# Context ahead through the mixer, the gated unit and the second feed-forward step of a fp32 trunk, with the latent's scan beside

## The chip, the cores and the metric

The kernel runs on one core of a Trainium2 chip. The core has a matrix engine (PE in the profile), a vector engine (DVE), a scalar engine (ACT), GpSimd (POOL) and a queue engine for transfers (SP). Each works through its own instructions in order; semaphores tie them together. The metric is device time of one execution in microseconds, median of three runs.

## The reference

A trunk of two layers for one sample: 512 latent tokens and 256 context tokens, width 1024, all in fp32. Each layer is a half feed-forward step, a token mixer and another half step; each part begins with an RMS norm whose scale, shift and gate come from a conditioning vector (the adaptive norm). The mixer of layer 0 is a diagonal state space model (S5) in both directions; that of layer 1 is gated linear attention (GLA).

```python
def ffn_half_step(x, w_norm, shift, scale, gate, w_in, w_out):
    h = rmsnorm(x, w_norm) * (1.0 + scale) + shift
    return x + 0.5 * gate * swiglu_ffn(h, w_in, w_out)
...
    yc_f, hf_re, hf_im = s5_direction(uc, *fwd, h0, h0)
    yc_b, hb_re, hb_im = s5_direction(jnp.flip(uc, 1), *bwd, h0, h0)
    yx_f, _, _ = s5_direction(ux, *fwd, hf_re, hf_im)
    yx_b, _, _ = s5_direction(jnp.flip(ux, 1), *bwd, hb_re, hb_im)
...
        z = jnp.einsum('bld,de->ble', jax.nn.gelu(y), w_glu.astype(F32)) + b_glu.astype(F32)
        val, gate = jnp.split(z, 2, axis=-1)
        return (val * jax.nn.sigmoid(gate)).astype(h.dtype)
```

The latent's scan starts from context's last states (`hf`, `hb`). Nothing goes from the latent to context before the GLA mixer, which needs both.

## The kernel before

**Layout.** The trunk (`xT`) lies with the width on 128 partitions in 8 tiles and the 768 tokens along the free dimension: 0 to 255 context, 256 to 767 latent. Every large product is three matmuls (`mm3`, L109): each operand is split into a rounded part and a rest (`hi`, `lo`), and hi*hi, lo*hi and hi*lo are summed. A weight tile of 512 KB is loaded by SP into `wraw` (4 buffers), cast on ACT into `whi` (L88, 5 buffers) and subtracted on DVE into `wlo` (L89, 5 buffers). The normed activation is kept split in `h`.

**Order.** A scheduler sets each engine's order from the order of the code and pool buffers; the code can hand a stage a list of *fillers*, pieces of other work that are issued between its units. `ffn` (L221) goes through 22 hidden units of 128: per unit a gate and a value product (16 `mm3` for each stretch of tokens), SiLU and their product, and in groups the output product. Two to three stretches of tokens share each weight. Adaptive-norm vectors come in 36 blocks of 2 MB of weights: one way on PE (`ten`, L394 and L401), one as a filler on DVE (`by_vector`, L422: `vec`, `rest`).

**The stages.** Loads; first half step of layer 0 (with the preparation of the S5 factors as fillers); S5; gated unit; second half step; first half step of layer 1; GLA; last half step; norm and store.

**S5.** The tokens are taken in runs of 8 (32 of context, 64 of the latent). `inputs` (L764) writes the normed input through DRAM (`U`). `states` (L796, matmuls L811) gives the state that each run adds. `scan` (L819, operations at L499) runs over the 96 runs on DVE: at each step the last state times the factors, and two additions, for each direction apart: 6 operations. `lagged` (L838, L851) adds what the tokens of a run give each other; its tables come from DRAM (`T`) and are cast on ACT (L845). `outputs` (L855) takes, for each of 8 tiles, copies of the states on ACT and DVE (L885, `xs`), 16 matmuls (L906) with a loaded factor (`O`), a sum (L908), a gelu (L910) and a store through DRAM (`Y`). `glu` (L916) loads Y (`yk`, 3 buffers), splits it (L931 on ACT, L932 on DVE) and makes 8 units of 16 `mm3` for each of two halves of 384 tokens. Nine adaptive blocks are made on PE around the scan (`ten`).

## Time and profile before

| what | value |
|---|---|
| median of 3 runs | 2896.99 us (2893.2 to 2899.43) |
| profiled execution, its own time | 2895.71 us |
| its span | 2893.9 us |
| PE busy | 95% of the span, mean granted clock 0.97 |
| DMA | 305.44 MB, mean 106 GB/s |

The page gives busy time by engine, the span in 40 slices of 72 us, the chain of work that ended last, and groups of instructions by line. The chain view names who was waited for. The timeline gives instructions with their start. A PE record's duration holds its way through the pipeline, so how fast products go is read from the distance of their starts. An fp32 matmul that is not split leaves two records, and a split one leaves one.

### The profile page before, as it was taken

To read this page: it belongs to the slowest core of one execution; us is meant where nothing else is said; L and a number is where in the kernel's file an instruction comes from. 1 tells how busy PE (TensorE), PEld (TensorE's weight loads), DVE (VectorE), ACT (ScalarE), POOL (GpSimd) and SP (SyncE) were. 2 spreads that over 40 slices of the span, in tenths; PEclk is the share of its full clock that TensorE was granted. 3 is DMA by queue.
4 is the path that set the end of the run, shared out by engine and by line. 5 is a ranking of instruction groups with operands and counts; after the bars stand their busy time and mean duration, and the time that the engine had idled before them with its cause. 6 is when DMAs were issued, how large, how long until landed. Compare 5 with 4: busy or idle time off the path is not lost.

```text
span 2893.9 us, 44979 instructions
## 1 busy us (share of the span) xinstructions
PE 2750.2 (95%) x18319; PEld 2589.0 (89%) x18319; DVE 1733.4 (60%) x3980; ACT 874.0 (30%) x1415; POOL 8.7 (0%) x41
## 2 busy tenths in 40 slices
PE   6999999996679999999999999999999899799997
PEld 5899999995479999999999999999998788788887
DVE  6689686536873564555527745575367786643434
ACT  4222222224572322111124221121255453422221
POOL 0000000000000000000000000000000000000000
PEclk9999999997789999999999999999999899899998
DMA  6445343517863133332321433343102111243320
GB/s 224 144 114 146 112 135 121 170 59 234 299 201 84 52 103 88 95 95 88 95 59 37 139 95 103 109 122 90 53 17 87 45 59 59 72 123 93 95 77 30
DMA packets 396044, 305.44 MB, mean 106 GB/s; under 512 B 57994, under 2 KB 344188, under 8 KB 395836
## 3 DMA queue, kind: packets, MB, share of 16 engines
q1 hardware_dynamic: 382908, 289.97, 33.7%
q10 hardware_dynamic: 12928, 12.59, 1.3%
q8 instruction: 144, 2.36, 0.4%
q14 instruction: 64, 0.52, 0.1%
HBM read 275.77 MB, written 30.41 MB: 106 GB/s over the span
## 4 chain that ended last, share of the span: by engine, by line
PE 90%; DVE 3%; DMA 3%; ACT 3%; issue 1%; SPq 0%; ACTq 0%; DVEq 0%
PE bank L113 27%; PE bank L114 27%; PE bank L115 27%; PE bank L811 1%; DMA wraw<-in_ffn_w_in_dram 1%; PE bank L1105 1%; PE bank L1104 1%; PE bank L1106 1%; PE aux L1237 1%; DVE big L499 1%; ACT xs L885 1%; PE aux L690 1%; DVE st L499 1%; PE bank L906 0%; PE bank L394 0%
## 5 line engine op out<-in xcount | busy, mean ns | idle before, releaser
L114 PE MATMUL bank<-h,whi 128*128 128x384 f32 (+3 forms) x3160 | 1048.8, 333 | 1.7 <-DVE h L932 1.7
L115 PE MATMUL bank<-h,wlo 128*128 128x384 f32 (+3 forms) x3160 | 1047.9, 332 | 0.0
L113 PE MATMUL bank<-h,whi 128*128 128x384 f32 (+3 forms) x3160 | 1044.5, 334 | 3.2 <-ACT whi L88 1.7
L88 ACT CAST whi<-wraw 128x1024 fp32r<-128x1024 f32 x313 | 327.7, 1048 | 992.3 <-PE bank L114 960.4
L113 PEld LDWEIGHTS bank<-h,whi 128*128 128x128 f32 (+1 forms) x3160 | 593.3, 189 | 24.7 <-issue 2.3
L114 PEld LDWEIGHTS bank<-h,whi 128*128 128x128 f32 (+1 forms) x3160 | 595.1, 188 | 20.0 <-DVE h L932 2.4
L115 PEld LDWEIGHTS bank<-h,wlo 128*128 128x128 f32 (+1 forms) x3160 | 593.4, 188 | 17.8 <-issue 0.8
L89 DVE TENSOR_TENSOR wlo<-wraw,whi 128x1024 fp32r<-128x1024 f32 x313 | 381.1, 1219 | 277.0 <-ACT whi L88 269.6
L114 PE MATMUL bank<-ml,whi 128*128 128x384 f32 (+2 forms) x1360 | 444.5, 328 | 0.0
L113 PE MATMUL bank<-mh,whi 128*128 128x384 f32 (+2 forms) x1360 | 442.7, 329 | 1.4 <-DVE er L503 1.4
L115 PE MATMUL bank<-mh,wlo 128*128 128x384 f32 (+2 forms) x1360 | 443.7, 328 | 0.0
L264 DVE TENSOR_TENSOR sg<-sg,bank 128x384 f32<-128x384 f32 (+2 forms) x166 | 89.5, 539 | 398.0 <-PE bank L115 385.1
L275 DVE SCALAR_TENSOR_TENSOR xT<-bank,hg,xT 128x256 f32<-128x256 f32 (+3 forms) x488 | 230.2, 500 | 154.4 <-PE bank L115 153.7
L113 PEld LDWEIGHTS bank<-mh,whi 128*128 128x128 f32 x1360 | 255.3, 188 | 8.5 <-issue 1.9
L115 PEld LDWEIGHTS bank<-mh,wlo 128*128 128x128 f32 x1360 | 255.6, 188 | 6.5 <-issue 0.2
L114 PEld LDWEIGHTS bank<-ml,whi 128*128 128x128 f32 x1360 | 255.6, 188 | 6.2
L422 DVE SCALAR_TENSOR_TENSOR adaacc<-wraw,cs,adaacc 128x512 f32<-128x512 f32 x266 | 187.4, 745 | 19.9 <-DMA wraw<-in_ada_w_dram 19.4
L265 ACT CAST mh<-sg 128x384 fp32r<-128x384 f32 (+2 forms) x166 | 83.5, 503 | 326.0 <-DVE sg L264 323.5
L263 ACT ACTIVATE sg<-bank 128x384 f32<-128x384 f32 (+2 forms) x166 | 79.5, 479 | 195.4 <-PE bank L115 195.3
L266 DVE TENSOR_TENSOR ml<-sg,mh 128x384 fp32r<-128x384 f32 (+2 forms) x166 | 89.7, 540 | 28.0 <-ACT mh L265 28.0
L150 ACT ACTIVATE sq<-xT 128x256 f32<-128x256 f32 (+1 forms) x126 | 52.9, 429 | 75.4 <-DVE xT L275 53.9
L151 DVE TENSOR_TENSOR ssq<-ssq,sq 128x256 f32<-128x256 f32 (+1 forms) x126 | 54.9, 437 | 30.6 <-ACT sq L150 27.9
(297 smaller groups left out, 2360.3 us busy)
## 6 DMA issues: line engine op xcount, KB each, us to landing
wraw<-in_ffn_w_in_dram SPq DMA_DIRECT2D x176, 512.0 KB, 3.8
wraw<-in_ada_w_dram SPq DMA_DIRECT2D x97, 512.0 KB, 3.7
wraw<-in_ffn_w_out_dram SPq DMA_DIRECT2D x88, 512.0 KB, 3.5
wraw<-in_gla_w_in_dram SPq DMA_DIRECT2D x24, 512.0 KB, 3.9
s5R<-s5r ACTq DMA_DIRECT2D x16, 512.0 KB, 2.6
s5O<-s5g SPq DMA_DIRECT2D x64, 128.0 KB, 2.4
wlo<-in_ada_w_dram SPq DMA_DIRECT2D x16, 512.0 KB, 10.9
wraw<-in_s_w_glu_dram SPq DMA_DIRECT2D x16, 512.0 KB, 4.8
```

The source lines that it names most:

```text
L88: nc.scalar.copy(out=hi[:, :n], in_=raw[:, :n])
L89: nc.vector.tensor_tensor(out=lo[:, :n], in0=raw[:, :n], in1=hi[:, :n].bitcast(F32), op=ALU.subtract)
L113: mm(out, wh, a[0], start=first, stop=False)
L114: mm(out, wh, a[1], start=False, stop=False)
L115: mm(out, wl, a[0], start=False, stop=last)
L263: nc.scalar.activation(sg, banks[0][:, :e - s], AF.Silu)
L264: nc.vector.tensor_mul(sg, sg, banks[1][:, :e - s])
L265: nc.scalar.copy(out=mh[:, o], in_=sg)
L266: nc.vector.tensor_tensor(out=ml[:, o], in0=sg, in1=mh[:, o].bitcast(F32), op=ALU.subtract)
L275: nc.vector.scalar_tensor_tensor(out=self.xT[:, d, a:z], in0=b[:, a - s:z - s], scalar=gate[i][:, d:d + 1], in1=self.xT[:, d, a:z], op0=AL ...
L422: nc.vector.scalar_tensor_tensor(out=acc[:, v], in0=w[:, k], scalar=col, in1=acc[:, v], op0=ALU.mult, op1=ALU.add)
L499: self.c.nc.vector.tensor_tensor(out=out, in0=a, in1=b, op=op)
```

## The change

1. **Tiles by kind.** `h`, and the scratch that shares its place, are two tiles each, for context (`h0`) and latent (`h1`). `at` picks the one. Stretches that mixed the two kinds, halves of 384, are now 256 and 512 tokens in all stages.
2. **Scan.** One step takes both directions at once: 3 operations, of 256 and twice 128 columns.
3. **Order.** Context's scan (31 steps) stands between the states of the two kinds; then come `lagged`, `outputs` of context, `glu` of context with three latent scan steps behind each of its 8 units, context's norm with two adaptive blocks on PE, and the second half step for context alone. Its fillers are 10 times four scan steps and the 8 pieces of the latent's outputs, whose `O` tiles have their own pool (`om`, 3 buffers). Then `glu` and half step for the latent alone, with the next norm of context as a filler.
4. **Weights.** Those of `glu` and of the second half step, and `O`, are loaded twice, and the former two also cast and subtracted twice.
5. **Adaptive blocks.** By vector in the first half step 8 instead of 4; on PE around S5 4 instead of 9; in the second half step 8 instead of 6; in layer 1's first half step 8 instead of 9.

```diff
-            for z in range(2):
-                def state(s, step=64):
-                    return fview(r, s * P + z * 32 + (64 if step < 0 else 0), [(step, 2), (1, 32)])
-                t = pool.tile([P, 2, 2, 32], F32, tag="st", name="st", bufs=4)
-                self.tt(t, fview(self.sa, z * 32, [(P, 2), (64, 2), (1, 32)]),
-                        state(s - 1).unsqueeze(1).to_broadcast([P, 2, 2, 32]), ALU.mult)
-                self.tt(state(s), state(s), t[:, 0], ALU.add)
-                self.tt(state(s, -64), state(s, -64), t[:, 1], ALU.add)
+            t = pool.tile([P, 2, 2, 64], F32, tag="st", name="st", bufs=2)
+            carry = [fview(self.r[1], o, [(64 - 2 * o, 2), (1, 64)]) for o in (0, 64)]
+            last = carry[0] if s == NX5 else state(s - 1)
+            self.tt(t, fview(self.sa, 0, [(P, 2), (64, 2), (1, 64)]), last.unsqueeze(1).to_broadcast([P, 2, 2, 64]), ALU.mult)
+            new = carry if s == NX5 - 1 else [state(s), state(s, -64)]
+            self.tt(new[0], state(s), t[:, 0], ALU.add)
+            self.tt(new[1], new[1], t[:, 1], ALU.add)
...
         for j in range(KT):
             ws.append([c.weight(wg[:, :, q * D + j * P:q * D + (j + 1) * P]) for q in range(2)])
-            if j < KT - 3:
-                for s, e in parts:
-                    step(j, ws[j], s, e)
+            if j < KT - nlast:
+                step(j, ws[j], *whole)
+            if j < len(work):
+                work[j]()
...
-        both, halves = (0, TOK), [(0, 384), (384, 768)]
+        both, halves = (0, TOK), [(0, CTX), (CTX, TOK)]
...
-            ada = [vec(0, m, q, sp) for m in (4, 3) for q in range(2)]
+            ada = [vec(0, m, q, sp) for m in (4, 3, 5, 7) for q in range(2)]
...
-            s5.scan(sp, NX5, N5)
-            ten(2)
             s5.lagged()
-            ten(2)
-            work = s5.outputs(sp, 3, yp, last)
-            ten(4)
-            work()
+            work = s5.outputs(0, sp, 3, core.spare)
+            ten(1)
+            for f in work:
+                f()
+        mods.scale(0, 2)
+        with pool("s5l") as sp, pool("s5m", "right") as mp:
...
+            def behind(s, e):
+                norm(0, 2, 1, 1)(s, e)
+                ten(2)
+                mods.half_gate(0, 1)
+            s5.glu(0, sp, [(0, CTX)], 0, behind, [lambda: steps(3)] * KT)
+            def beside():
...
+                return [lambda: steps(4)] * 10 + s5.outputs(1, sp, 1, unit)
+            ffn(0, 1, (0, CTX), [(0, CTX)], [(0, CTX)], [(0, CTX)], mp, beside)
...
-            s5.glu(yp, halves, thirds, norm(0, 2, 12))
+            with pool("s5y", "right") as yp:
+                s5.glu(1, yp, lat, 3, norm(0, 2, 12))
             with pool("mid") as mp:
-                ffn(0, 1, both, thirds, halves, thirds, mp,
-                    lambda: rest(6, mp) + [lambda: (mods.scale(1, 0), mods.half_gate(1, 0))], norm(1, 0))
+                ffn(0, 1, (CTX, TOK), lat, [(CTX, TOK)], lat, mp,
+                    lambda: rest(8, mp) + [lambda: (mods.scale(1, 0), mods.half_gate(1, 0)),
+                                           lambda: norm(1, 0, 7, 3)(0, CTX)], norm(1, 0))
```

In the rows below, each is a line of the program, an operation, the tile written and the tiles read, and the shape; lines of the changed kernel differ by some 7 from those before (the scan's operations are L499 before and L506 after, the casts L88 and L89 in both).

DVE, in the scan, before: each step is two products (`st`) and four additions into the state (`big`), with nothing else between them here.

```order
L499 TENSOR_TENSOR st<-s5sa,big 128x128 x2
L499 TENSOR_TENSOR big<-big,st 128x2x32 x4
L499 TENSOR_TENSOR st<-s5sa,big 128x128 x2
L499 TENSOR_TENSOR big<-big,st 128x2x32 x4
L499 TENSOR_TENSOR st<-s5sa,big 128x128 x2
```

DVE, after, in context's second half step (L271 and L273 are its gating, `s` the latent's states):

```order
L89 TENSOR_TENSOR wlo<-wraw,whi 128x1024
L506 TENSOR_TENSOR s_6382<-s_6382,st 128x128
L271 TENSOR_TENSOR sg<-sg,bank 128x256
L506 TENSOR_TENSOR s_6382<-s_6382,st 128x2x64
L506 TENSOR_TENSOR st<-s5sa,s_6382 128x256
L89 TENSOR_TENSOR wlo<-wraw,whi 128x1024
L506 TENSOR_TENSOR s_6382<-s_6382,st 128x128
L273 TENSOR_TENSOR ml<-sg,mh 128x256
L506 TENSOR_TENSOR s_6382<-s_6382,st 128x2x64
L506 TENSOR_TENSOR st<-s5sa,s_6382 128x256
```

The scan's three operations now stand between the subtractions and gatings on which that stage's products wait.

PE, after, where the gated unit of context has ended and its second half step begins (L401: adaptive blocks, here `wraw`, `whi` and `wlo` hold their weights; L171 and L190: the norm's sum and spread):

```order
L401 MATMUL bank<-wraw,cs 32x512 x2
L401 MATMUL bank<-whi,cs 32x512 x2
L401 MATMUL bank<-wlo,cs 32x512 x2
L408 MATMUL aux<-quarter,adar 128x2 x8
L171 MATMUL aux<-ones,ssq 128x1 x2
L190 MATMUL bank<-ident,rs 128x128 x2
L113 MATMUL bank<-h_8302,whi 128x256 x4
L114 MATMUL bank<-h_8302,whi 128x256
```

Before, PE went straight from the last output matmuls (L906) to the gated unit, and the blocks stood ahead of both. Now the blocks and the norm stand between two stages of products, in one queue.

ACT, after, later in that half step (L896: copies of the latent's states; L910: gelu; L270 and L272: gating):

```order
L88 CAST whi<-wraw 128x1024
L272 CAST mh<-sg 128x256
L896 COPY xs_9228<-s_6382 64x4x64 x8
L910 ACT_TABLE_LOAD
L910 ACTIVATE y_10983<-y_10983 128x512
L74 DMA s5Y_846<-y_10983 128x8x64
L270 ACT_TABLE_LOAD
L270 ACTIVATE sg<-bank 128x256
L88 CAST whi<-wraw 128x1024 x2
```

The latent's output pieces have moved in between the casts and gatings of this stage, with a change of the function table on either side of the gelu.

More of the change, by code (lines that the diff above doesn't have):

```diff
@@ L49, in __init__ @@
         self.tmp = stack.enter_context(tc.tile_pool(name="tmp", bufs=1))
-        self.queue = []
-        self.ones = self.const.tile([P, P], F32, name="ones")
+        self.queue, self.h = [], [None, None]
+        self.ones = self.const.tile([P, 1], F32, name="ones")
         nc.vector.memset(self.ones, 1.0)
@@ L484, in __init__ @@
         self.U = [dram.tile([KT, P, L5, n], F32, name=f"s5U{i}") for i, n in enumerate((NX5, N5 - NX5))]
-        self.Y = dram.tile([KT, P, L5, N5], F32, name="s5Y")
+        self.Y = [dram.tile([KT, P, L5, n], F32, name=f"s5Y{i}") for i, n in enumerate((NX5, N5 - NX5))]
     def small(self, name):
@@ L708, in turn_k @@
         def turn_k():
-            b, k = c.aux(), pool.tile([P, 256], F32, tag="s5k", name="s5kt", bufs=1)
+            b, k = c.aux(), c.tmp.tile([P, 384], F32, tag="nt", name="s5kt", bufs=2)[:, :256]
             for z in range(2):
@@ L853, in lagged, with outputs @@
                 nc.scalar.copy(out=u.rearrange("p g n -> p (g n)"), in_=b[:, :4 * N5])
-    def outputs(self, pool, ahead, yp, last):
-        c, nc, r = self.c, self.c.nc, self.r
-        loaded, self.ys = {}, []
+    def outputs(self, kind, pool, ahead, unit):
+        c, nc, r = self.c, self.c.nc, self.r[kind]
+        n0, n = ((0, NX5), (NX5, N5 - NX5))[kind]
+        loaded = {}
         def load(kt):
-            om = [c.spare() for _ in range(2)]
+            om = [unit() for _ in range(2)]
             for z in range(2):
@@ L867, in outputs @@
             loaded[kt] = load(kt)
-        xs = [pool.tile([P, 2, 8, N5], F32, name=f"xs{i}", tag=f"xs{i}", bufs=1) for i in range(2)]
-        for x in xs:
-            nc.gpsimd.memset(x[:, 0, :, 0:1], 0.0)
-        def states(kt, s0, s1, copies):
+        xs = [pool.tile([P, 2, 8, n], F32, name=f"xs{i}", tag=f"xs{i}", bufs=1) for i in range(2)]
+        if kind == 0:
+            for x in xs:
+                nc.gpsimd.memset(x[:, 0, :, 0:1], 0.0)
+                nc.gpsimd.memset(x[:, 1, :, n - 1:n], 0.0)
@@ L889, in outputs @@
-        early = 80
-        with c.tc.issue_after(last.ins):
-            for kt in range(2):
-                states(kt, 0, early, [nc.scalar.copy] * 2)
-        def work():
-            for kt in range(KT):
-                x = xs[kt % 2]
-                om = loaded.pop(kt) if kt in loaded else load(kt)
-                states(kt, early if kt < 2 else 0, N5, [nc.scalar.copy, nc.vector.tensor_copy])
-                y = pool.tile([P, 8, N5], F32, tag="y5", name="y5", bufs=4)
-                for h in range(2):
-                    b = c.bank()
-                    for i in range(4):
-                        g = 4 * h + i
-                        o = b[:, i * N5:(i + 1) * N5]
-                        for z in range(2):
-                            nc.tensor.matmul(o, om[z][:, g * P:(g + 1) * P], x[:, z, g], start=(z == 0), stop=(z == 1))
-                    yh = y[:, 4 * h:4 * h + 4].rearrange("p g n -> p (g n)")
-                    nc.vector.tensor_tensor(out=yh, in0=b[:, :4 * N5], op=ALU.add,
-                                            in1=self.u[kt][:, 4 * h:4 * h + 4].rearrange("p g n -> p (g n)"))
-                    nc.scalar.activation(yh, yh, AF.Gelu_apprx_tanh)
-                c.store(dview(self.Y, kt * P * TOK, [(N5, P), (C5 * TOK, 8), (1, N5)]), y)
-                if 0 < kt < 4:
-                    self.load_y(yp, kt - 1)
@@ L914, in outputs @@
-        return work
-    def glu(self, pool, parts, last, after):
+                    for z in range(2):
+                        at, step, to = (count - 1, -P, 0) if z else (0, P, n - count)
+                        src = fview(r, at * P + a * 64 + z * 32 + 4 * kt, [(1, 4), (step, count)], 64 * g, 64)
+                        dst = fview(x, z * 8 * n + g * n + to, [(2 * n, 4), (1, count)], 64 * a, 64)
+                        (nc.vector.tensor_copy if z and not kind else nc.scalar.copy)(out=dst, in_=src)
@@ new lines, in piece @@
+        def piece(kt):
+            x = xs[kt % 2]
+            om = loaded.pop(kt) if kt in loaded else load(kt)
+            states(kt)
+            y = pool.tile([P, 8, n], F32, tag="y5", name="y5", bufs=2)
+            b = c.bank()
+            for g in range(8):
+                for z in range(2):
+                    nc.tensor.matmul(b[:, g * n:(g + 1) * n], om[z][:, g * P:(g + 1) * P], x[:, z, g],
+                                     start=(z == 0), stop=(z == 1))
+            nc.vector.tensor_tensor(out=y, in0=b[:, :8 * n].rearrange("p (g n) -> p g n", g=8), op=ALU.add,
+                                    in1=self.u[kt][:, :, n0:n0 + n])
+            nc.scalar.activation(y, y, AF.Gelu_apprx_tanh)
+            c.store(dview(self.Y[kind], kt * P * L5 * n, [(n, P), (C5 * L5 * n, 8), (1, n)]), y)
@@ L1099, in proj_v @@
             b = c.bank()
-            ts = slice(t * P, (t + 1) * P)
+            s, e = t * P, (t + 1) * P
             for k in range(KT):
@@ L1490, in hybrid_trunk @@
         factors = held.enter_context(pool("s5c"))
-        blocks = [(0, m, q) for m in (5, 7, 6, 8) for q in range(2)] + \
+        blocks = [(0, m, q) for m in (6, 8) for q in range(2)] + \
                  [(1, m, q) for m in (1, 0, 2, 4, 3, 5, 7, 6, 8) for q in range(2)]
```

127 lines of the change are left out of this document (64 added, 63 removed).

## The prediction

> **What bounds the kernel now.** I read the busy totals first, then the 40 slices, then the chain of work that ended last, then windows by stage.
>
> ```profile
> PE 2750.2 (95%) x18319; PEld 2589.0 (89%) x18319; DVE 1733.4 (60%) x3980; ACT 874.0 (30%) x1415; POOL 8.7 (0%) x41
> PE   6999999996679999999999999999999899799997
> PE 90%; DVE 3%; DMA 3%; ACT 3%; issue 1%; SPq 0%; ACTq 0%; DVEq 0%
> ```
>
> PE carries 90% of the chain and is full in every slice but the first, three from 650 us on, and a few late ones. So time can be won in the holes, and everything added to a full stage is paid in full. The windows (columns: stretch; busy us of PE, of PE's weight loads, of DVE, ACT and POOL with counts; granted clock; DMA share; GB/s) size them:
>
> ```profile
> 100.00:640.00 540.00, 538.62 (x3458) 525.11 (x3457) 390.65 (x919) 127.31 (x197) 3.69 (x7) 1.00 0.44 127
> 640.00:870.00 230.00, 164.45 (x2417) 137.06 (x2417) 172.09 (x782) 135.81 (x218) 1.47 (x12) 0.81 0.75 233
> 848.00:870.00 22.00, 18.62 (x90) 17.51 (x89) 20.29 (x24) 18.72 (x25) 0.00 (x0) 0.84 1.02 282
> 1060.00:1540.00 480.00, 480.00 (x2838) 478.11 (x2837) 243.51 (x405) 96.65 (x144) 0.00 (x0) 1.00 0.30 88
> ```
>
> The hole is the S5 mixer. The timeline gives its ends: the last matmul of the first feed-forward step, the first and last scan operation, and the first matmul of the gated unit.
>
> ```profile
> 660.65 0.28 PE L115 MATMUL bank<-mh,wlo 128*128 128x256 f32 x1
> ...
> 700.55 0.29 DVE L499 TENSOR_TENSOR st<-s5sa,big 128x128 f32<-128x128 f32 x1 [0.33 <-ACT big L816]
> ...
> 810.26 0.23 DVE L499 TENSOR_TENSOR big<-big,st 128x64 f32<-128x64 f32 x1
> ...
> 847.80 0.42 PE L113 MATMUL bank<-h,whi 128*128 128x384 f32 x1
> ```
>
> 847.8 - 660.65 = 187 us pass without a wide product. In the 22 us behind it PE is busy 18.62 at a clock of 0.84, some 15.6 of full-speed work, so another 6 go: **193 us**. The scan takes 110 of them.
>
> **The scan.** Both directions in one operation: 3 per step where there were 6.
>
> ```profile
> L499 DVE TENSOR_TENSOR big<-big,st 128x64 f32<-128x64 f32 x380 | 60.3, 214 | 0.8 <-ACT big L816 0.5
> L499 DVE TENSOR_TENSOR st<-s5sa,big 128x128 f32<-128x128 f32 x190 | 46.1, 280 | 2.3 <-ACT big L816 2.2
> ...
> 661.75 0.41 DVE L151 TENSOR_TENSOR ssq<-ssq,sq 128x256 f32<-128x256 f32 x1
> ```
>
> The timeline merges and overlaps these operations by about 0.08 us: 190 of 0.28 and 380 of 0.214 fill 95 steps at 2 x 0.20 + 4 x 0.135 = 0.94 us. The new step is one operation of 256 columns (0.41 - 0.08 = 0.33) and two of 128 (0.20 each): 0.73 us. Context's 31 steps are 23 us, the latent's 64 are 47.
>
> **The hole after the change.** Context's path no longer holds the latent's 64 steps nor five of nine adaptive-norm blocks, but it still holds the context states (until 700.55), the lag products and context's outputs.
>
> ```profile
> 713.17 10.27 DMA wraw<-s5T
> ...
> 752.31 7.23 PE bank L851 x48
> ...
> 846.97 0.39 PE L906 MATMUL bank<-xs,wraw 128*128 128x96 f32 x2
> 847.19 0.39 PE L906 MATMUL bank<-xs,whi 128*128 128x96 f32 x2
> ...
> s5Y<-y ACTq DMA_DIRECT2D x8, 384.0 KB, 6.5
> yk<-s5Y SPq DMA_DIRECT2D x8, 384.0 KB, 4.6
> u<-s5U SPq DMA_DIRECT2D x7, 128.0 KB, 4.6
> ```
>
> The lag products end at 759.5 now, behind the loads of the lag tables and their ACT copies. With less adaptive-weight traffic they may end at 750; I take 755. Context's 128 output matmuls follow at 0.22 each (two rows start 0.22 apart, one matmul of two records), 28.2 us, to 783. Then add and gelu (1 us), the store of Y (between 4.6, as 128 KB take, and 6.5; taken 4.6), its load (4.6) and the split (about 1.4) give 795. The gated unit's first unit takes its operand tiles one by one, so seven eighths of its 5.7 us run before: effective 790, plus 2 for the low clock at the start. The hole is then 792 - 660.65 = 131 us: **-62**. Bounds: at before's output pace (40 us from 808 to 848, 5 per tile instead of 3.5) and lag products at 759.5 it is -46; with lag products at 745 and the Y transfers half hidden, -77.
>
> **Latent outputs inside full PE.** They go from the hole into context's feed-forward step: 128 matmuls of 64 columns, while the 128 of 32 stay. The trace shows no 64 column case. From above it is bounded by the 0.22 of 96 columns, from below by one column:
>
> ```profile
> 1550.82 0.50 PE L163 MATMUL aux<-ones,ssq 128*128 128x1 f32 x4
> 1551.17 0.69 PE L182 MATMUL bank<-ident,rs 128*128 128x128 f32 x4
> ```
>
> Four records of one column take 0.35 us, 0.09 each, where 96 columns take 0.11: width hardly counts. I take the upper end: **+28** (bounds 22 and 28). The Trainium skill, "TensorE: Matmul & The Clock Gate", section LDWEIGHTS, says that loading a 128-column stationary tile takes 128 / 1.2 GHz, 107 ns, whatever else the matmul does. The trace agrees with 0.09 to 0.11 per record. If cost went with moved columns instead, the split would be free and this term 28 x 64 / 96 = 19.
>
> **Products at other widths.** Gated unit and second step run context and latent apart, 256 and 512 columns, and other stages drop 384.
>
> ```profile
> 619.81 0.34 PE L115 MATMUL bank<-h,wlo 128*128 128x384 f32 x1
> 619.98 0.34 PE L113 MATMUL bank<-h,whi 128*128 128x384 f32 x1
> ...
> 625.93 0.28 PE L114 MATMUL bank<-ml,whi 128*128 128x256 f32 x1
> 626.05 0.28 PE L115 MATMUL bank<-mh,wlo 128*128 128x256 f32 x1
> ```
>
> Starts lie 0.175 apart for 384 columns and 0.118 for 256, both 0.46 ns a column: 0.
>
> **Junction 1, gated unit to feed-forward on context.** Nothing else fills PE here. The sum over the last unit, square sums, the reciprocal root, its spread and the first tile's split follow one another, and PE's queue holds 16 products of two adaptive blocks ahead of the norm's. The trace has one bare norm, at the end of the second step: products stop with the rows just shown, at 1550.8, and start again at 1555.1:
>
> ```profile
> 759.53 3.59 PE bank L394 x32
> ...
> 1555.12 1.43 PE L113 MATMUL bank<-h,whi 128*128 128x256 f32 x5 [0.27 <-ACT h L218]
> ```
>
> so 5 us is the least. On top come the blocks (their 32 records took 3.6 us at 759.5), their weights, which wait for gated-unit slots, and scan operations between the norm's on DVE: **+12** (5 to 22). That old bubble goes, since context's norm is now done beside the latent's products: **-5**.
>
> **Junction 2, feed-forward on context to the latent's gated unit.** The first load of the latent's Y overlays the mid tiles, so on SP it waits for the last matmul of context's step. Three buffers serve eight tiles: load 4.6, split 1.16 + 1.08,
>
> ```profile
> L931 ACT CAST h<-yk 128x512 fp32r<-128x512 f32 x8 | 9.3, 1159 | 0.0
> L932 DVE TENSOR_TENSOR h<-yk,h 128x512 fp32r<-128x512 f32 x8 | 8.6, 1080 | 0.3 <-ACT h L931 0.3
> ```
>
> 6.8 us a round, three rounds and 1.1 for the last tile, then 1.4 us of products: 22 us for the first unit, which needs 48 x 0.233 = 11.2. **+10** (5 to 18). Queued behind these loads on SP are the unit's other weights, but nine are ahead.
>
> **Pace of context's feed-forward step.** Each weight serves 256 columns only. Per unit of 72 products (8.5 us), PE needs three casts on ACT and three subtractions on DVE.
>
> ```profile
> L88 ACT CAST whi<-wraw 128x1024 fp32r<-128x1024 f32 x313 | 327.7, 1048 | 992.3 <-PE bank L114 960.4
> L89 DVE TENSOR_TENSOR wlo<-wraw,whi 128x1024 fp32r<-128x1024 f32 x313 | 381.1, 1219 | 277.0 <-ACT whi L88 269.6
> L885 ACT COPY xs<-big 64x320 f32<-64x320 f32 x8 | 6.0, 745 | 3.2 <-DVE big L499 3.1
> L885 ACT COPY xs<-big 64x196 f32<-64x196 f32 x8 | 4.1, 518 | 0.2
> L910 ACT ACT_TABLE_LOAD x1 | 1.3, 1283 | 0.0
> L910 ACT ACTIVATE y<-y 128x384 f32<-128x384 f32 x16 | 8.4, 527 | 3.1 <-DVE y L908 1.6 <-DVE xs L885 1.4
> ```
>
> In the first ten units DVE has 3 x 1.14, four steps of 0.73 and some four operations of 256 columns at 0.33 for gating and sums, 7.7 us: it fits barely. Later each output piece stands 69 products apart, 8.1 + 3.5 = 11.6 us of PE; ACT has 2.9 casts (3.0), eight copies of 256 columns (between 0.52 and 0.745, taken 0.63: 5.0), two table switches (2.6), gelu of 512 columns (0.527 for 384, so 0.7) and three gating operations of some 0.4: 12.5. Eight pieces fall 0.9 behind each: **+7** (0 to 34). DMA stands at about 1.5 MB per 8.5 us, under the 233 GB/s of the hole. Four more adaptive blocks by vector in the first step are 50 us of DVE, beside 390 busy in 540: 0; were a weight late behind one, at most 1 us each. Two more in the second step: DVE 243 of 480, 0.
>
> **Sum**: -62 + 28 + 12 - 5 + 10 + 7 = -10, 2895.7 - 10 = 2886 for the profiled execution; the median stands 1.3 above that, so **2887**.
>
> **Rivals.** *ACT bounds the outputs (slower).* In ACT's queue the copies for piece k+2 wait for the matmuls of piece k, gelu for DVE's sum, and casts stand behind both. If that round trip (3.5 + 0.7 us) is exposed at each piece, the term is 8 x 4.2 = 34, not 7: 2914. It is slower than before once a piece falls 2.1 us behind (the forecast has 0.9), by over 6 us at 2.9. For it: ACT has no slack there. Against: five cast buffers, 14 us of products. *The hole doesn't shrink as said.* If lag tables and output weights, and not the scan, set it, it keeps the 5 us per tile and 759.5: 16 us more, 2903; with half of that, 2895. For it: DMA share 0.75 and a 10.27 us wait. Against: seven blocks less to load. *The junctions are covered.* Slots free early, ACT and DVE keep pace: -62 + 28 + 5 - 5 + 5 + 0 = -29, 2868; with -77 for the hole, 2853. For it: my junction terms are made of latencies added up; against: the waits are in the queues' order.
>
> **Chances.** Forecast 0.38 (own range 2874 to 2891), covered junctions 0.18, hole not shrunk 0.18, ACT 0.26. A measurement of this kernel tells 0.2%, some 6 us, from no change. The forecast and the covered case are faster; of the unshrunk hole most lies within 6 us: faster 0.56, same 0.17, slower 0.27. The range runs from the covered case's low end to somewhat over ACT's 2914: 2852 to 2920.
>
> **What would show it.** After: first products of the gated unit near 790; L906 of 64 columns at 0.22 in a PE that stays full; a stop of about 12 us near 837 and of about 7 near 1070, then a slow unit; no stop before the third step. Wrong if PE stutters through context's step, or if the first products come after 800 or before 775.

## The result, and the profile after

The changed kernel is slower: **2959.64 us** (median of 4 runs, 2958.07 to 2963.65) against 2895.09 (4 runs, 2890.96 to 2899.43), a ratio of 1.0225 with a 95% interval of 1.0206 to 1.0244. Forecast were 2887 us and a range up to 2920. The profiled execution is the slowest of the four, 2963.65 us, span 2961.9.

The page of the changed kernel, busy totals, the slices of PE and of its granted clock, and the shares of the chain of work that ended last:

```profile
PE 2808.1 (95%) x18495; PEld 2458.2 (83%) x18495; DVE 1856.3 (63%) x3747; ACT 992.5 (34%) x1555; POOL 7.5 (0%) x33
PE   6999999996988998999999999999999999799997
PEclk7999999997688999999999999999999899899998
PE 87%; DVE 5%; DMA 3%; ACT 2%; issue 2%; SPq 0%; DVEq 0%; ACTq 0%
```

PE has the same share of the span and yet is 58 us more busy in sum. The slices show where: the hole near 700 us has narrowed from three slices under 9 (6, 6, 7) to one (6), but the clock around it is low in four slices (7, 6, 8, 8) where it was in three (7, 7, 8), and three later slices of PE, from 815, 889 and 1111 us, have an 8. The windows show the first step, the hole, ten microseconds inside the hole, the junction to context's second step, and the rest of that step (columns as before):

```profile
100.00:640.00 540.00, 537.61 (x3401) 455.29 (x3402) 427.05 (x950) 125.74 (x190) 3.68 (x7) 0.99 0.50 146
676.00:830.00 154.00, 120.98 (x2008) 113.02 (x2008) 71.50 (x206) 79.85 (x143) 0.22 (x4) 0.67 0.71 207
780.00:790.00 10.00, 10.00 (x49) 10.00 (x48) 1.60 (x5) 2.04 (x6) 0.00 (x0) 0.50 0.30 73
870.00:910.00 40.00, 27.54 (x199) 23.09 (x197) 34.67 (x100) 17.41 (x27) 0.00 (x0) 0.83 0.54 172
1000.00:1138.00 138.00, 127.88 (x1015) 127.49 (x1015) 62.22 (x88) 93.79 (x125) 0.00 (x0) 0.91 0.65 194
```

The third row is the one to learn from. PE is busy 10 of 10 us, DVE, ACT and the queues are nearly idle, and only 49 records go through: 0.20 us each, at a clock of 0.50. A full PE is not a fast PE.

**Where the time went.** The wide products (L113 to L115) are the same in both kernels, 13800 records. I weighed each with the spacing of starts at full clock (0.118 us for 256 columns, 0.1755 for 384, 0.233 for 512), so that both kernels hold 2329 us of products, and read off both traces when a given amount of them was done.

| place | products done | before, us | after, us | after minus before |
|---|---|---|---|---|
| first product | 0 | 51.3 | 60.8 | +9 |
| near the end of the first half step | 550 | 654.5 | 670.3 | +16 |
| behind the hole | 558 | 853.7 | 829.3 | -24 |
| gated unit of context nearly done | 600 | 898.0 | 873.6 | -24 |
| behind junction 1 | 620 | 917.8 | 921.4 | +4 |
| ten units into context's second step | 700 | 999.3 | 1000.9 | +2 |
| behind junction 2 | 790 | 1089.3 | 1146.5 | +57 |
| into the latent's second step | 900 | 1199.8 | 1265.9 | +66 |
| behind the old bubble | 1300 | 1608.6 | 1673.6 | +65 |
| last product | 2329 | 2868.0 | 2935.4 | +67 |

The hole gave 40 us (from +16 to -24). Everything else in the S5 layer took: 16 in the first step, 28 at junction 1, 55 in the second part of context's step and at junction 2, 9 at the latent's norm. Behind 1266 us nothing of size happens. The 9 at the first product are at the top of a scatter: the experiments that keep this start have their first product at 57.3 to 59.8, that is 6 to 9 later than before.

### The profile page after: what moved, and what is told of

It reads as the page before. It is cut to its first block, busy times and chain, and to the rows that moved or that the text cites. A ratio compares the mean times of both kernels' runs of the same rounds, so it can differ in the third digit from the quotient of the medians.

```text
span 2961.9 us, 45516 instructions
## 1 busy us (share of the span) xinstructions
PE 2808.1 (95%) x18495; PEld 2458.2 (83%) x18495; DVE 1856.3 (63%) x3747; ACT 992.5 (34%) x1555; POOL 7.5 (0%) x33
## 4 chain that ended last, share of the span: by engine, by line
PE 87%; DVE 5%; DMA 3%; ACT 2%; issue 2%; SPq 0%; DVEq 0%; ACTq 0%
PE bank L113 25%; PE bank L114 25%; PE bank L115 25%; PE bank L906 3%; DVE wlo L89 1%; PE bank L819 1%; DMA om<-s5O 1%; PE aux L1236 1%; DMA wraw<-in_ffn_w_in_dram 1%; PE bank L190 1%; PE bank L1104 1%; PE bank L1105 1%; PE bank L1103 1%; DMA yk<-s5Y 1%; PE bank L401 1%
## 5 line engine op out<-in xcount | busy, mean ns | idle before, releaser
L113 PE MATMUL bank<-h,whi 128*128 128x256 f32 (+2 forms) x3160 | 1042.8, 335 | 18.8 <-ACT h L930 14.0
L114 PE MATMUL bank<-h,whi 128*128 128x256 f32 (+2 forms) x3160 | 1047.4, 333 | 0.1
L115 PE MATMUL bank<-h,wlo 128*128 128x256 f32 (+2 forms) x3160 | 1046.4, 333 | 0.8 <-DVE wlo L89 0.8
L88 ACT CAST whi<-wraw 128x1024 fp32r<-128x1024 f32 x395 | 412.0, 1048 | 1134.3 <-PE bank L114 1025.4
L89 DVE TENSOR_TENSOR wlo<-wraw,whi 128x1024 fp32r<-128x1024 f32 x395 | 480.7, 1219 | 339.3 <-ACT whi L88 326.1
L113 PEld LDWEIGHTS bank<-h,whi 128*128 128x128 f32 (+1 forms) x3160 | 594.1, 190 | 86.8 <-ACT h L930 14.8
L115 PEld LDWEIGHTS bank<-h,wlo 128*128 128x128 f32 (+1 forms) x3160 | 595.6, 189 | 64.3 <-DVE wlo L89 1.0
L114 PE MATMUL bank<-ml,whi 128*128 128x256 f32 (+1 forms) x1360 | 451.3, 334 | 1.3 <-DVE ml L273 1.3
L115 PE MATMUL bank<-mh,wlo 128*128 128x256 f32 (+1 forms) x1360 | 448.4, 332 | 0.0
L113 PE MATMUL bank<-mh,whi 128*128 128x256 f32 (+1 forms) x1360 | 443.9, 334 | 4.1 <-ACT mh L272 3.9
L282 DVE SCALAR_TENSOR_TENSOR xT<-bank,hg,xT 128x256 f32<-128x256 f32 (+1 forms) x368 | 213.8, 595 | 173.6 <-PE bank L115 172.5
L113 PEld LDWEIGHTS bank<-mh,whi 128*128 128x128 f32 x1360 | 259.5, 192 | 30.4 <-ACT mh L272 4.1
L115 PEld LDWEIGHTS bank<-mh,wlo 128*128 128x128 f32 x1360 | 260.7, 192 | 25.9 <-issue 0.6
L271 DVE TENSOR_TENSOR sg<-sg,bank 128x256 f32<-128x256 f32 (+1 forms) x166 | 89.6, 540 | 266.4 <-PE bank L115 256.5
L272 ACT CAST mh<-sg 128x256 fp32r<-128x256 f32 (+1 forms) x166 | 83.7, 504 | 202.8 <-DVE sg L271 202.0
L270 ACT ACTIVATE sg<-bank 128x256 f32<-128x256 f32 (+1 forms) x166 | 79.2, 477 | 105.1 <-PE bank L115 104.9
L273 DVE TENSOR_TENSOR ml<-sg,mh 128x256 fp32r<-128x256 f32 (+1 forms) x166 | 89.7, 541 | 18.3 <-ACT mh L272 18.3
```

Of the source, the lines that this page charges most:

```text
L88: nc.scalar.copy(out=hi[:, :n], in_=raw[:, :n])
L89: nc.vector.tensor_tensor(out=lo[:, :n], in0=raw[:, :n], in1=hi[:, :n].bitcast(F32), op=ALU.subtract)
L113: mm(out, wh, a[0], start=first, stop=False)
L114: mm(out, wh, a[1], start=False, stop=False)
L115: mm(out, wl, a[0], start=False, stop=last)
L270: nc.scalar.activation(sg, banks[0][:, :e - s], AF.Silu)
```

## The experiments

Ratios are against the kernel before, run beside on the same chip, whose median was 2894 to 2896 each time. The edits are against the changed kernel unless said otherwise, and "better" is against its 2959.64. A stretch "from 600 to 620" is one between two amounts of products done, as in the table. Runs that change nothing in a stretch still scatter there: the hole is 144.5 to 151.5 us long, 600 to 620 takes 44.4 to 49.5, 650 to 790 takes 190 to 198.

### The clock in the hole

**Wider output matmuls.** Context's 128 output matmuls of 32 columns get 128 columns by repeating the moving operand four times, in two banks of four; DVE takes the first 32 of each.

```diff
-                    nc.tensor.matmul(b[:, g * n:(g + 1) * n], om[z][:, g * P:(g + 1) * P], x[:, z, g],
+                        nc.tensor.matmul(b[:, i * w * n:(i + 1) * w * n], om[z][:, g * P:(g + 1) * P],
+                                         fview(x, (z * 8 + g) * n, [(0, w), (1, n)]) if w > 1 else x[:, z, g],
```

> The changed kernel, with the 128 output matmuls of context taking their 32 columns four times over (128 columns, three quarters of the result unused). In the changed kernel each of their 256 records takes 0.21 us at a granted clock of 0.50, where the 96-column ones of before took 0.11 at 0.95. Theory A (the narrow moving operand keeps the granted clock at half, and the weight load runs at that clock): four times the columns bring the clock to about 1.0 after a few us, a record to 0.11 to 0.13, and the kernel gets 20 to 28 us faster, about 2935. Rival B (the loads of the output factors or the copies pace this stage): records stay 0.21 or longer, the kernel is the same or slower.

Measured: 2932.15 us, 1.0126 (1.011 to 1.0142), 27.5 us less than the changed kernel. The timeline of PE, two neighbouring rows in the changed kernel:

```profile
780.37 0.61 PE L906 MATMUL bank<-xs,whi 128*128 128x32 f32 x2
780.80 0.61 PE L906 MATMUL bank<-xs,wraw 128*128 128x32 f32 x2
```

and in this experiment, with its window below:

```profile
775.14 0.39 PE L910 MATMUL bank<-xs,wraw 128*128 128x128 f32 x2
775.36 0.39 PE L910 MATMUL bank<-xs,whi 128*128 128x128 f32 x2
780.00:790.00 10.00, 10.00 (x90) 9.85 (x89) 6.63 (x14) 7.14 (x14) 0.00 (x0) 1.00 0.71 188
```

0.43 us a matmul has become 0.22 with four times the columns. The granted clock is 1.00 instead of 0.50, and 90 records go through in the 10 us instead of 49. The hole, from the last product of the first step to the first of the gated unit, shrinks from 149.6 us to 131.0. The low clock, and not the number of matmuls, made the outputs slow. The other 9 of the 27.5 us lie outside the hole, in stretches that scatter by as much.

**Twice the width.** The same with w = 2, in one bank.

```diff
-            w = 1 if kind else 4
+            w = 1 if kind else 2
```

> The changed kernel with context's output matmuls taking their 32 columns twice (64 columns). With 32 the granted clock stays at 0.50, with 128 it rises. Theory A (the clock follows the share of time in which columns move: at 64 it is still too low): records stay near 0.21 us, no gain. Rival B (64 are enough, as the latent's pieces of 64 ran at 0.11 us each between wide products): records at 0.11, some 25 us faster.

Measured (two executions only): 2953.32 us, 1.02 (1.0179 to 1.022), 6 better, but not in the hole, which is no shorter (151.3 us). The window:

```profile
780.00:790.00 10.00, 10.00 (x48) 10.00 (x48) 3.20 (x10) 4.00 (x10) 0.00 (x0) 0.50 0.31 77
```

64 columns leave the clock at 0.50. Before the change the outputs had 96, in a PE that was busy for only 80% of the window, at 1.00:

```profile
830.00:840.00 10.00, 7.94 (x65) 7.31 (x64) 8.57 (x22) 9.40 (x14) 0.44 (x2) 1.00 0.88 247
```

They had begun at the half clock, back to back, and went over to the full one at 814 us. The timeline of PE in the kernel before, on both sides:

```profile
812.61 0.63 PE L906 MATMUL bank<-xs,whi 128*128 128x96 f32 x2
813.04 0.64 PE L906 MATMUL bank<-xs,wraw 128*128 128x96 f32 x2
...
814.19 0.39 PE L906 MATMUL bank<-xs,wraw 128*128 128x96 f32 x2
814.42 0.39 PE L906 MATMUL bank<-xs,whi 128*128 128x96 f32 x2
```

So it is the width that matters, not that PE is full: back to back, 96 columns bring the clock up here and 64 don't hold it.

### The scan

**Merged scan alone.** The kernel before, its scan with both directions at once.

```diff
-            for z in range(2):
...
+            t = pool.tile([P, 2, 2, 64], F32, tag="st", name="st", bufs=2)
```

> The kernel before, with only the scan's two directions put in one operation (3 operations per step instead of 6). Steps of 0.73 us instead of 0.94 (95 steps: 20 us less on DVE). Theory A (scan sets the hole): the hole shrinks by 10 to 20 us, 2876 to 2886. Rival B (nine adaptive blocks on PE, whose last products end at 805 just ahead of the first output matmul at 807.87, set it as much as the scan): under 5 us, 2890 to 2896.

Measured: 2900.97 us, 1.0018 (1.0009 to 1.0028): about 5 slower than before, which neither theory had. The timeline of DVE, one step:

```profile
772.72 0.43 DVE L499 TENSOR_TENSOR st<-s5sa,big 128x256 f32<-128x256 f32 x1
773.18 0.62 DVE L499 TENSOR_TENSOR big<-big,st 128x128 f32<-128x128 f32 x2
773.84 0.42 DVE L499 TENSOR_TENSOR st<-s5sa,big 128x256 f32<-128x256 f32 x1
```

A step takes 1.12 us, where six operations took 0.94 and the prediction said 0.73. With two directions apart, an operation on one direction starts 0.08 us before the other's record has ended. In the merged step each operation reads what the one ahead of it wrote: starts lie 0.46 apart at a duration of 0.425, so nothing overlaps. The 95 longer steps are 17 us more on DVE, of which 5 reach the kernel.

**Two chains in the changed kernel.** Its scan in six operations again.

```diff
-            t = pool.tile([P, 2, 2, 64], F32, tag="st", name="st", bufs=2)
...
+            for z in range(2):
...
+                t = pool.tile([P, 2, 2, 32], F32, tag="st", name="st", bufs=4)
```

> The changed kernel with the scan again as two chains, 6 operations a step, in the changed order. In the profile of the changed kernel each of the three operations starts only when the one before it has ended (0.46, 0.33 and 0.33 us apart, 1.11 a step), while before, with two chains taking turns, starts were 0.20 and 0.135 apart, 0.94 a step. Theory A (the merged operations are one dependent chain and pay its latency, 0.17 us a step): context's 31 steps and the norm after the gated unit get 5 to 10 us shorter, about 2952. Rival B (the scan is covered everywhere in the changed kernel): within 3 us of 2960.

Measured: 2963.65 us, 1.0235 (1.0217 to 1.0254): no gain. Context's 31 longer steps lie beside the lag products and the loads, the latent's beside products. What is a loss in the old order is covered in the new one.

**No scan steps in the gated unit.** They follow in context's feed-forward step, five at a time.

```diff
-            s5.glu(0, sp, [(0, CTX)], 0, behind, [lambda: steps(3)] * KT)
+            s5.glu(0, sp, [(0, CTX)], 0, behind, [])
...
-                return [lambda: steps(4)] * 10 + s5.outputs(1, sp, 1, unit)
+                return [lambda: steps(5)] * 13 + s5.outputs(1, sp, 1, unit)
```

> The changed kernel without scan steps behind the gated unit's units of context; the 64 steps of the latent all stand in the feed-forward step (13 fillers of 5). Between 600 and 620 us of wide products the changed kernel loses 28 us against before. Theory A (scan operations stand between the root's operations on DVE, which is why these take 5 us): 5 to 8 us are won there, and 3 to 10 lost in the feed-forward step, where DVE then has 5 steps of 1.11 per unit. Rival B (the blocks' weights and the casts behind them set the norm's place): nothing is won there.

Measured: 2957.14 us, 1.0213 (1.0196 to 1.023). The stretch from 600 to 620 of products takes 50.3 us, not less than the changed kernel's 47.8. Scan operations between those of the norm are not what makes junction 1 long.

### The first step and the start

**First norm in three stretches.** The kernel before, with one edit of the start. The changed kernel has it: with the stretches 256 and 512, its first norm runs over three stretches of 256.

```diff
-            for s, e in halves:
+            for s, e in thirds:
                 core.norm_split(s, e, mods.pair(mods.sc[0][0]), mods.shift(0, 0), 1)
```

> The kernel before, with only the first norm taken in thirds instead of halves. In the changed kernel the first wide product starts at 60.8 instead of 51.3. Theory A (the thirds do it, since the third stretch's sums and root operations stand in DVE's order between those of the first): plus 7 to 10 us, about 2904. Rival B (it is the other layout of the scratch that the first adaptive weights are loaded into): within 2 us of before.

Measured: 2916.0 us, 1.0072 (1.0057 to 1.0087), 20 slower: 9 at the first product, 3 more by 100 us of products, 6 in the hole, 4 behind 1800 us of products. Each stretch has its own chain of square sum, root and spread, and the last one stands ahead of the first product. The timeline of PE in the changed kernel shows two such rounds, 5.1 us apart:

```profile
54.75 0.85 PE L190 MATMUL bank<-ident,rs 128*128 128x128 f32 x3
59.89 1.22 PE L190 MATMUL bank<-ident,rs 128*128 128x128 f32 x4 [4.29 <-DVE rs L183]
60.76 0.56 PE L113 MATMUL bank<-h,whi 128*128 128x256 f32 x1
```

**Only context's norm ahead of the first product.**

```diff
-            core.ensure()
+            core.ensure(CTX)
```

> The changed kernel, in which the first norm's second and third stretch may be spread behind the first products (the queue of delayed norm parts is emptied for context's stretch only before the first feed-forward step). In the changed kernel PE has the spread of the third stretch (L190, 59.89 us) ahead of the first wide product (60.76), against 51.3 before. Theory A (PE's queue order holds the first product until the third stretch's root is done): the first product starts near 53, 5 to 8 us faster, about 2954. Rival B (DVE's shared work on all three stretches sets it): under 3 us.

Measured: 2952.66 us, 1.0196 (1.0181 to 1.0211), 7 better by the median, but the first product comes at 56.2, only 1 to 4 earlier than in the runs without the edit (57.3 to 59.8). The two runs with several mends, further down, have the same edit and nothing else at the start, and there it comes at 52.7 and 53.0, as theory A said, against 51.3 before. So the order of the third stretch can give back most of the start's loss; why it gave less here is open.

**Eight vector blocks alone.** The kernel before, with 8 adaptive blocks by vector in the first step and 4 on PE around S5.

```diff
-            ada = [vec(0, m, q, sp) for m in (4, 3) for q in range(2)]
+            ada = [vec(0, m, q, sp) for m in (4, 3, 5, 7) for q in range(2)]
...
-                if i % 14 == 13 and ada:
+                if i % 7 == 6 and ada:
...
```

> The kernel before, with the change's shift of adaptive blocks alone: 8 instead of 4 by vector in the first feed-forward step, 4 instead of 9 on PE around the scan, 7 instead of 6 in the second step; scan as before. Theory A (the hole of before ends with the scan, 810 us, and the blocks are hidden in it): within 4 us of before, with up to 5 lost in the first step. Rival B (the blocks' loads of 2 MB each delay lag tables and output factors): 5 to 12 us faster, about 2888.

Measured: 2905.06 us, 1.0036 (1.0023 to 1.0049): 9 slower, 5.6 of it in the first step and 5 in the hole, although five of nine PE blocks had left the hole. On the average DVE has room, being busy for 427 of 540 us in the changed kernel; that it has none at single units is what the next run shows.

**Ten vector blocks, none at junction 1.**

```diff
-            ada = [vec(0, m, q, sp) for m in (4, 3, 5, 7) for q in range(2)]
+            ada = [vec(0, m, q, sp) for m in (4, 3, 5, 7, 8) for q in range(2)]
...
-                ten(2)
                 mods.half_gate(0, 1)
```

> The changed kernel without the two adaptive blocks on PE between context's gated unit and its feed-forward step; they are made by DVE in the first feed-forward step (10 blocks there). In the changed kernel PE has 20 us of holes from 876 to 915. Theory A (the blocks and their weight loads are on that path): 8 to 15 us faster, 2945 to 2952. Rival B (the norm's own chain on DVE, between scan steps and subtractions, sets it): under 4 us, and what DVE has more to do in the first step costs up to 5.

Measured: 2989.21 us, 1.0325 (1.031 to 1.034): 30 slower than the changed kernel. The stop of PE at junction 1 is 12.4 us instead of 18.0, and the stretch from 600 to 620 takes 43.1, but the first step loses 32. Its last vector block comes too late; of the waits of that step (waiter, releaser; us in all, times, the longest) one row, and the window at 540 us:

```profile
PE aux L440 <- DVE adas L435: 25.3, 2, 20.4
540.00:560.00 20.00, 0.74 (x17) 0.40 (x17) 17.81 (x33) 0.37 (x1) 0.00 (x0) 0.51 0.80 245
```

PE stands for 20 us behind a block's small product while DVE works 17.81 of 20: what "DVE 390 busy in 540" could not tell.

### Junction 1

**The two blocks behind two units of context's step.** They are fillers of the step instead of standing ahead of its norm's products in PE's queue.

```diff
                 norm(0, 2, 1, 1)(s, e)
-                ten(2)
-                mods.half_gate(0, 1)
...
+                return [lambda: ten(1)] * 2 + [lambda: mods.half_gate(0, 1)] + [lambda: steps(4)] * 10 + s5.outputs(1, sp, 1, unit)
+            ffn(0, 1, (0, CTX), [(0, CTX)], [(0, CTX)], [(0, CTX)], mp, beside, early=3)
```

> The changed kernel with the two adaptive blocks on PE moved from ahead of context's norm to behind the first two units of its feed-forward step. Between 600 and 620 us of wide products the changed kernel loses 28 us; without the blocks at all it lost 23, without scan steps 30. Theory A (what is left is that the blocks' 4 MB of weights are fetched ahead of the step's first weights, whose casts at 881 then hold DVE's subtractions and the norm): 8 to 15 us faster, about 2948. Rival B (the norm's chain alone sets it, its weights come in its shadow): within 5 us.

Measured: 2952.17 us, 1.0194 (1.0172 to 1.0217), 7.5 better; the stretch from 600 to 620 takes 40.6 instead of 47.8. The timeline of PE in the changed kernel, from the last product of context's gated unit to the first of its second step:

```profile
875.15 0.28 PE L115 MATMUL bank<-h,wlo 128*128 128x256 f32 x1
...
883.01 1.19 PE L408 MATMUL aux<-quarter,adar 128*128 128x2 f32 x8 [1.63 <-ACT adar L405]
884.09 1.01 PE L171 MATMUL aux<-ones,ssq 128*128 128x1 f32 x4
890.86 1.22 PE L190 MATMUL bank<-ident,rs 128*128 128x128 f32 x4 [5.75 <-DVE rs L183]
893.19 0.58 PE L113 MATMUL bank<-h,whi 128*128 128x256 f32 x1 [1.11 <-ACT h L226]
```

and with the blocks moved:

```profile
867.31 0.28 PE L115 MATMUL bank<-h,wlo 128*128 128x256 f32 x1
870.27 0.61 PE L171 MATMUL aux<-ones,ssq 128*128 128x1 f32 x4 [2.67 <-DVE ssq L159]
874.83 1.20 PE L190 MATMUL bank<-ident,rs 128*128 128x128 f32 x4 [3.95 <-DVE rs L183]
877.14 1.23 PE L113 MATMUL bank<-h,whi 128*128 128x256 f32 x4 [1.11 <-ACT h L226]
```

18.0 us without a product have become 9.8 (10.3 and 10.5 in the two later runs with this edit). The bare norm is these 9.8: the square sums (2.67), the root (3.95), the spread and the split. How much of the 8 us is kept is less sure: the blocks now hold the step's first units, and in the two later runs 600 to 620 takes 44.1 and 44.8, no less than in some runs without the edit. In the old bubble at 1550 us the spread came 0.35 us behind a row of square sums, where the root between them takes 3.95 here: its root was done already, and that row showed half a norm.

### The latent's outputs

**One factor for all eight pieces.** 14 of 16 loads of `O` go; the outputs are made with the first factor.

```diff
         def load(kt):
+            if kind and one:
+                return one
```

> The changed kernel in which the latent's output pieces load their factor once and use it for all eight tiles (14 of 16 loads of 512 KB left out, so the latent's values are not the reference's). In the changed kernel PE waits some 16 us for these loads (longest 5.4), three buffers for two tiles a piece. Theory A (these waits are on PE's path): 13 to 20 us faster, about 2944. Rival B (ACT, with copies, gelu, table switches and casts, is as late as the loads): under 6 us.

Measured: 2949.88 us, 1.018 (1.016 to 1.0199): 10 better, 13 by the trace between 650 and 790 of products. The timeline of PE in the changed kernel shows such a wait:

```profile
1045.00 3.68 PE L906 MATMUL bank<-xs,om 128*128 128x64 f32 x32
...
1054.03 0.33 PE L906 MATMUL bank<-xs,om 128*128 128x64 f32 x2
1059.76 6.66 PE L906 MATMUL bank<-xs,om 128*128 128x64 f32 x30 [5.40 <-DMA om<-s5O]
1066.18 0.56 PE L113 MATMUL bank<-mh,whi 128*128 128x256 f32 x1
```

These are the third and the fourth piece. The third takes 3.5 us, as forecast, in a full PE. The fourth waits 5.4 us for its second factor tile, in three buffers that hold one piece and a half; in the wait the clock falls, and then the piece runs at half clock, 6.4 us. Summed over the eight stops between two products in which a piece stands, the pieces take 45.0 us in the changed kernel and 28.9 with one factor, eight times 3.61.

**Half of the latent's output matmuls.** The sum leaves out its second half.

```diff
-                for z in range(2):
+                for z in range(1 + (kind == 0)):
```

> The changed kernel with one of the two directions left out of the latent's output matmuls (64 instead of 128; the latent's values are not the reference's). Theory A (PE is full in context's feed-forward step and pays each): 64 x 0.22 = 14 us faster, about 2946. Rival B (ACT, or the loads, pace the pieces): under 5 us.

Measured: 2937.74 us, 1.0153 (1.0138 to 1.0168): 22 better. Half of the 28 us of matmuls explains 14. The rest is what the waits and the low clock had added: here no piece waits, and the eight stops are 1.82 each, 14.6 in sum. Of the 30 us that the pieces win, 20 are left at 790 of products.

**Y loads not held by the last matmul of context's step.** The tiles get buffers of their own, and the latent's gated unit starts inside the pool of the step.

```diff
-        y = pool.tile([P, L5, (NX5, N5 - NX5)[kind]], F32, tag="yk", name="yk", bufs=3)
+        y = pool.tile([P, L5, (NX5, N5 - NX5)[kind]], F32, tag=("yk", "y5")[kind], name="yk", bufs=3)
...
             ffn(0, 1, (0, CTX), [(0, CTX)], [(0, CTX)], [(0, CTX)], mp, beside)
+            s5.glu(1, sp, lat, 2, norm(0, 2, 12))
```

> The changed kernel with the latent's Y loaded into the buffers of the gelu's results, so that its first loads no longer wait for the last matmul of context's step (the last two instead of three units of the latent's gated unit run by stretches). In the changed kernel PE stands 5.7 us from 1138.05 and the first unit then stutters, 6.5 us lost in all. Theory A (the overlay costs this): 4 to 7 us faster, about 2954. Rival B (the last store of Y, itself late by the loads of factors, ends just then): under 2 us.

Measured: 2949.95 us, 1.0195 (1.0178 to 1.0211): 10 better by the median, 7 by the trace at junction 2, of which 3 go back at the latent's norm. In the changed kernel the stop there is

```profile
1138.05 0.28 PE L115 MATMUL bank<-mh,wlo 128*128 128x256 f32 x1
1143.76 1.65 PE L113 MATMUL bank<-h,whi 128*128 128x512 f32 x3 [5.43 <-ACT h L930]
```

5.7 us, then a few products at half pace. In the experiment no stop over 1.8 us is left there.

### Mends together

**Wide outputs, later third, later blocks** (the edits of the three runs above, merged scan):

```diff
+            w = 1 if kind else 4
...
+            core.ensure(CTX)
...
+                return [lambda: ten(1)] * 2 + [lambda: mods.half_gate(0, 1)] + [lambda: steps(4)] * 10 + s5.outputs(1, sp, 1, unit)
```

> The changed kernel with three mends that each won alone: output matmuls of 128 columns (27 us), the first norm's later stretches spread (7), the adaptive blocks behind the first two units (7); the scan stays merged. Theory A (the gains add; the two-chain scan, which the scheduler put ahead of the latent's state copies, took them back in the run with all): 2916 to 2922. Rival B (they overlap): 2928 to 2935.

Measured: 2932.44 us, 1.0127 (1.0111 to 1.0144). The sum of the three gains was 42; together they give 27, no more than the wide outputs alone.

**These, the two chains, and the factors in half tiles with six buffers:**

```diff
+                om = [unit() for _ in range(4)]
+                for i in range(4):
+                    c.dma(om[i], self.O[kt][i % 2][:, i // 2 * 512:(i // 2 + 1) * 512])
...
-                    return sp.tile([P, UNIT], F32, tag="om", name="om", bufs=3)
+                    return sp.tile([P, 512], F32, tag="om", name="om", bufs=6)
```

> The changed kernel with all that the runs point to: context's output matmuls at 128 columns (27 us won alone), the scan as two chains, the first norm's later stretches spread, the adaptive blocks behind the first two units, and the latent's output factors in six halves of tiles instead of three tiles. If the gains add: 2960 - 27 - 3 - 6 - 10 - 6 = 2908, still above before (2896), since the latent's outputs inside full PE (28 us) and the second loading stay. Rival: the gains overlap, since a later junction waits for the same loads: 2920.

Measured: 2933.44 us, 1.0135 (1.012 to 1.015). The window of this kernel at 720 us and two rows of the waits from 715 to 745 show a new hold:

```profile
720.00:740.00 20.00, 6.40 (x130) 6.11 (x128) 19.64 (x119) 11.37 (x17) 0.00 (x0) 0.72 0.39 106
ACT xs L908 <- DVE s L506: 8.4, 1, 8.4
PE bank L819 <- ACT s L824: 11.3, 2, 10.0
```

DVE runs context's scan without a break and PE is a third busy. ACT stands for 8.4 us at the copies of context's states, which wait for the scan, and PE for 10.0 at the latent's state products, whose copies come from the same ACT. The half tiles did what they were for: the latent's eight pieces take 33.6 us, against 45.5 with the three mends; but the hole is 141.5 us against 136.1. Nothing tried beats the kernel before.

## Why the prediction was wrong

The frame held: holes can be won, and what enters a full stage is paid. Of the terms, by the table of places:

| term | forecast | by the traces | tested by |
|---|---|---|---|
| first step and start | 0 | +16 | first norm in thirds, later third, vector blocks |
| hole of S5 | -62 | -40 | widths |
| junction 1 | +12 | +28 | blocks moved, no steps |
| context's step: latent outputs and pace | +35 | about +47 | one factor, half outputs |
| junction 2 | +10 | about +6 | early Y |
| latent's norm | not named | +9 | not tried |
| old bubble | -5 | -1 | not tried |
| rest of the program | 0 | +2 | not tried |
| sum | -10 | +67 | |

1. **The hole.** The step that failed is "context's 128 output matmuls follow at 0.22 each ... 28.2 us, to 783". From their first to their last they took 53 us. The chain view of the changed kernel gives their stretch in three rows (start, us, what, records; two records are a matmul, and L408 belongs to an adaptive block):

```profile
764.79 3.02 PE bank L906 x26
767.81 1.61 PE aux L408 x8
769.42 48.70 PE bank L906 x228
```

The first 26 records stand 0.112 apart, the forecast's 0.22 a matmul, with the same 32 columns; then the clock falls, and the rest stand 0.213 apart to the end. So the argument "width hardly counts" is right at full clock, the clock of the rows that it came from. What it left out is that a PE with nothing but narrow matmuls loses that clock, and that was the cost: 128 columns keep it, and the gain up to 600 us of products is then 62, as forecast. That the hole's length is then the forecast's 131 to the microsecond is in part luck: in that run too the outputs began 6 us earlier than said (88.7 us behind the first step's end instead of 94.3), and from the last of them to the first product passed 4 more. The prediction had quoted the Trainium skill, "TensorE: Matmul & The Clock Gate", for the load of the stationary tile; the same page, in Part 1, says that the clock is full after about 3.4 us of sustained work. The trace does not agree for these matmuls: back to back for 48.7 us, at 0.50 the whole time.

2. **The scan.** 0.73 us a step was wrong by half, and the gain by its sign too: a step takes 1.12, where it took 0.94 before. The working took an overlap between independent operations for a property of the operation. The merged scan cost 5 us in the old order and nothing in the new.

3. **Junction 1.** The least of 5 us was read from half a norm; a whole one is 9.8. The two blocks ahead of it lengthen the stop by 8 (shown by moving them in three runs), the scan operations by nothing (shown). The rest is argued from rows: a split pace of one tile in 1.2 us behind the norm, and a second stop of 4.2 us at 906.1 for the rounded part of the gated hidden unit (`mh`), which ACT makes behind a change of its function table and casts of weights.

4. **Context's step.** The matmuls cost 3.5 us a piece and the latent's scan steps beside products cost nothing (from +4 to +2 between 620 and 700), both as said. Missing were the waits for the loads of `O` with the low clock behind them: 16 us in the pieces (45.0 against 28.9), of which the one-factor run won 10 by its median. The rival "ACT bounds the outputs" named this stage, but not the engine: its waits are for DMA.

5. **Edits taken for free.** The norm in thirds was not named in the prediction at all; it is the 9 us at the first product (both kernels with it have 60.8). Four more vector blocks were set at 0 by an average, DVE 390 busy in 540; alone they cost 5.6 in the first step. The latent's norm, a junction like the first, was not counted: PE stops from 1234.9 to 1242.6. And the old bubble has not gone: where it was 4.4 us, a stop of 3.4 stands at 1636.3.

6. **Junction 2** was a little better than said, by the same working, whose sum is 22.9 for the first unit and not 22.

The miss of 77 us is 22 in the hole, 16 each in the first step and at junction 1, 12 in context's step, 9 at the latent's norm, 6 in bubble and rest, less 4 at junction 2. Even with the clock mended, 36 us stay.

**Open**: why the gains do not add. With three mends together the hole is 145.6 us long by nominal work against 140.5 with wide outputs alone, junction 1 takes 44.7, as with the wide outputs alone (44.6), where the moved blocks had given 40.6, and 750 to 790 loses 5 more. That fits a stage in which DVE, ACT and queue order bound in turn, but no run isolates it. The price of the first norm in thirds is open between about 7 and 20.

## What to carry to other kernels

Before small matmuls are laid alone into a hole, look for a row of the same width and the same neighbours and read its clock: the busy share does not show it. Cutting work in two by data (context first, the rest beside) makes each junction appear twice, and each costs a whole norm, a restart of weights and its clock; count them all before the gain of the hole is booked. A merged operation is only cheaper if the parts were not covering each other's latency, and an edit hidden "on the average" wants the unit in which it runs, not the stage.

## What the runs showed of the hardware

- **Clock and width.** fp32 matmuls of 32 or 64 moved columns, back to back, began at full clock with 0.11 us a record, were granted 0.50 after 3 to 6 us, and then took 0.21 for as long as they ran; 128 columns kept 1.00 and 0.11, and 96, begun at 0.50, came to 1.00 after 5 us. Inside a stream of wide products, 32 records of 64 columns took 3.5 us, full pace; behind a wait of 5.4 us, 30 took 6.4.
- **Dependent vector operations.** An addition or product of 256 columns that reads the result of the one ahead starts 0.034 us after that one's recorded end (0.46 apart at 0.425); independent ones of 64 and 128 columns started 0.08 before it. Between the two lies 0.11 us, a quarter of the 0.46.
